# A trunk layer on one core: unit phases from two small tables, and the embedding, the first weight loads and a branch's number arranged anew around the routing

## The chip, the cores and the metric

The kernel runs on one core of one Trainium2 chip. The metric is the device time of one execution in microseconds (us). The profile is of one execution, and its times count from the start of that execution's span.

## The reference

One post-norm decoder layer for 512 tokens of 2048 features, in float32:

```python
z = x @ w_in + b_in                      # 2048 -> 1024 (u) + 1024 (v) + 1024 (g)
y_ssm = s5_group(u, lam, dt, b, c, d_skip, w_glu, b_glu)   # 64 groups, 64 complex states each
y_conv = conformer_conv_group(v, g, w_dw, ...)             # 31 taps per channel, LN, silu
y = concat([y_ssm, y_conv]) @ w_o + b_o
h = layer_norm(ALPHA * x + y, ln1_g, ln1_b)
m = hierarchical_moe(h, w_rg, w_re, w_gate, w_up, w_down)  # 32 experts, 2 per token
h = layer_norm(ALPHA * h + m, ln2_g, ln2_b)
e = (p @ w_p) * sigmoid(h @ w_pg + b_pg)                   # p: 512 x 256
x = layer_norm(ALPHA * h + e, ln3_g, ln3_b)
```

The state-space part is the recurrence s(t) = lam_bar * s(t-1) + B u(t) with complex lam_bar for each state, and y = Re(C s) + d_skip * u. The kernel works on it in blocks of 8 tokens: within a block it multiplies with tables of powers of lam_bar, and across the 64 blocks it scans the magnitudes alone, after the block states have been turned by unit phases exp(-i n theta), and turns them back behind the scan. `cc` and `ss` are the cosines and sines of these phases for block numbers n = 0..63.

## The kernel before, in words

The program is written in the order of its stages, and a planner reorders the instructions of each engine: it puts them on the engines by their waits and by costs that it assumes, so what stands next to what is its doing. Tiles come from pools; a new tile waits until the last reader of the buffer it takes is done.

Stages, in the profile's time:

- 0 to about 402: `x @ w_in` in 24 column tiles. Every float32 product is made of three matmuls of split operands (high x high, low x high, high x low; L100 to L102), for which ScalarE casts the high part (L79) and VectorE or GpSimd subtracts for the low part (L80). Eight SSM tiles of 128 channels, with their state-space work, alternate with tiles of the convolution, whose 31 taps run on VectorE (L234, L236). GpSimd makes the SSM tile's tables (`ssm_tables`, L439 to L454, with a scratch tile `big` of 128x1024). VectorE makes the phases: `phases(ft)` (L401 to L419) runs once for two SSM tiles and doubles six times, from 1 block number to 64; each doubling is six products or sums of 128x(8m) elements, m = 1, 2, 4 up to 32. For each tile ScalarE copies the half it needs into `pc` and `pz` (L496, L498), and VectorE multiplies with them around the scan (L525 to L534).
- 402 to 470: `w_glu`. The SSM outputs and the conv outputs went to DRAM (`z_dram`, `c_dram`) and are read back as `zraw` and `hcv`, on SP's queue.
- 470 to 677: `w_o`, LN1, and the logits of the router for the four token tiles (`logits`, L848 and L852). `tt` holds the four token tiles of h, which are also stored to `h_dram`.
- 677 to 733: `embedding()` computes p @ w_p for all tokens (L835), copies it on ScalarE (L836) and stores it to `p_dram` for the last stage (L838). It needs nothing from the layer, so it stands beside the last logits. Then the routing, in small VectorE instructions and matmuls (L950 to L1027): `cmax`, the number of rows that an expert has beyond the usual, goes into `tab`; slots and weights of the rows come from one-hot sums (L190, L196, L203).
- 726 to 1272: the experts, in 13 groups. A group gathers its rows of h from DRAM (GpSimd, L1059), transposes them (L1073), multiplies by gate and up weights (L1093), forms the activation, multiplies by the down weights (L1113) and scatters the result (L1063). The weights of an expert are 6 blocks of 1 MB (4 `w_gu`, 2 `w_dn`), 192 in all, loaded on SP's queue into a ring of 17 buffers (L1055), of which the last two are the `raw` buffers of the stages before. Group 0 has two fixed experts, 12 blocks; which experts the others have is read from `ids` into SP's registers (L1127). Behind group 0 stands a branch on `most` (the value of `cmax`, L1159), for the rows that don't fit; it isn't taken here.
- 1272 to the end: LN2, the gate product `h @ w_pg`, times `p_dram`, LN3.

Each DMA that SP or ScalarE issues takes the next of eight completion counters (lanes) in program order, and waits until the last transfer on that lane has landed. At a branch, SP waits for all eight.

Of the kernel before, what the change touches and what calls it, by code (L numbers as in the profile page):

```python
# [17 lines left out]
P = 128  # L18
# [36 lines left out]
def build(tc, I, out, dbg=None, stages=9):  # L55
# [188 lines left out]
    def bank(name, bufs=1):  # L244
        if name in bturn:

            n = bturn[name]
            bturn[name] += 1
            name, bufs = (("zp", 4) if n % 5 < 4 else ("xp", 1)) if name == "ops" else (("wps", "cps")[n % 2], 1)
        return psA.tile([P, 512], FT, name=name, tag=name, bufs=bufs)  # L250

    if True:
        with ExitStack() as s2:
# [136 lines left out]

            Cb = tpool.tile([P, 8, 4, 6], FT, name="Cb")
            Sb = tpool.tile([P, 8, 4, 6], FT, name="Sb")
            for dst, srct in ((Cb, cs), (Sb, sn)):
# [4 lines left out]

            def phases(ft):

                cc = tpool.tile([P, 8, NN], FT, name="cc")  # L401
                ss = tpool.tile([P, 8, NN], FT, name="ss")
                tm = vpool.tile([P, 8, NN // 2], FT, name="tm", tag="xr", bufs=1)
                G.memset(cc[:, :, 0:1], 1.0)
                G.memset(ss[:, :, 0:1], 0.0)
                bases = [t[:, ft:ft + 2].rearrange("p t g j -> p (t g) j") for t in (Cb, Sb)]
                for j in range(6):
                    m = 1 << j
                    cb_, sb_ = (b[:, :, j:j + 1].broadcast_to([P, 8, m]) for b in bases)
                    t_ = tm[:, :, 0:m]  # L410
                    c0, c1, s0, s1_ = cc[:, :, 0:m], cc[:, :, m:2 * m], ss[:, :, 0:m], ss[:, :, m:2 * m]
                    V.tensor_tensor(c1, c0, cb_, op=OP.mult)
                    V.tensor_tensor(t_, s0, sb_, op=OP.mult)
                    V.tensor_tensor(c1, c1, t_, op=OP.subtract)
                    V.tensor_tensor(s1_, s0, cb_, op=OP.mult)
                    V.tensor_tensor(t_, c0, sb_, op=OP.mult)
                    V.tensor_tensor(s1_, s1_, t_, op=OP.add)
                return cc, ss

            cs_pair = []  # L420
            setup.close()
# [3 lines left out]
            def ssm_tables(ft):  # L425
# [208 lines left out]
    if True:  # L634
# [146 lines left out]
        with ExitStack() as s3:  # L781
# [40 lines left out]

            def embedding():

                pT = wB.tile([P, 2, S], FT, name="pT", tag="whi", bufs=4)
                nc.sync.dma_start(pT, I["pT"])
                for q in range(2):
                    wp = raw_load(I["w_p"][q]).rearrange("p (k n) -> p k n", k=2)
                    for c in range(2):
                        for m in range(NT):  # L830
                            if m % 2 == 0:
                                pe_ = wB.tile([P, 2, 512], FT, name="pe", tag=("whi", "wlo")[m // 2], bufs=4)
                            ps = bank("ops")
                            for k in range(2):
                                T.matmul(ps, pT[:, k, m * P:(m + 1) * P], wp[:, k, c * 512:(c + 1) * 512], start=k == 0, stop=k == 1)  # L835
                            A.copy(pe_[:, m % 2], ps)  # L836
                            if m % 2:
                                A.dma_start(p_dram[m - 1:m + 1, 2 * q + c].rearrange("m p d -> p m d"), pe_)  # L838

# [37 lines left out]
            for c in range(4):  # L877
# [19 lines left out]
                else:  # L897
                    hls = [next(w_o) for q in range(2)]
                    for m in range(NT):
# [3 lines left out]
                        last = finish(m)  # L903
            embedding()

# [131 lines left out]
    if True:  # L1037
# [98 lines left out]

        early = [loads(0, q) for q in range(6)]
        for m in range(NT):
            A.mul(tt[m], tt[m], ALPHA)
# [3 lines left out]
        for i, (width, members) in enumerate(GROUPS):  # L1143
# [4 lines left out]
            for q in range(4):  # L1148
                up(gu, st, loads(i, q) if i else early[q], q)
            at = act(gu, wt0[:, i:i + 1])  # L1150
            if i + 1 < NGR and i:
                columns()
            for q in range(2):
                down(at, st, loads(i, 4 + q) if i else early[4 + q], q, sl0[:, NGR + i:NGR + i + 1])
# [282 lines left out]
```

## Time and profile before

| | us |
|---|---|
| median of 3 runs (range) | 1529.64 (1523.28 to 1530.3) |
| the profiled execution | 1528.31 |
| its span | 1526.6 |
| TensorE busy | 1260.8 |
| VectorE busy | 825.5 |
| ScalarE busy | 371.6 |
| GpSimd busy | 332.8 |
| DMA, mean over the span | 229 GB/s |

The busy time of an engine is a sum over stages in which different things set the end: the table says which engine has most to do, and not which one is waited for. For that the rows further down are taken by stretch of time, and the waits of an engine name what ended each of them. The engines are PE (TensorE), DVE (VectorE), ACT (ScalarE), POOL (GpSimd) and SP, which only issues transfers here; PEclk is the granted TensorE clock as a share of 2.4 GHz.

### The profile page before, as it was taken

What the parts mean: (1) busy time and instruction counts of PE and PEld (TensorE: products, weight loads), DVE (VectorE), ACT (ScalarE), POOL (GpSimd) and SP (SyncE); (2) the same over time, 40 slices, a digit from 0 to 9 for tenths busy, and PEclk for the clock granted to TensorE, in tenths of its full rate; (3) what the DMA queues carried; (4) which work ended last, traced back from release to release, by engine and by line L of the source; (5) the groups of instructions that cost most, each with busy time, mean ns of one, the idle gap of its engine ahead of it and who ended that gap; (6) DMA issues with size and microseconds to landing.
All of it is one profiled execution on the core that took longest, in us unless ns stands there. A gap on an engine that the chain in (4) does not pass through costs nothing. (4 is left out here: it accounts for less than half of the span.)

```text
span 1526.6 us, 16736 instructions
## 1 busy us (share of the span) xinstructions
PE 1260.8 (83%) x6206; PEld 806.8 (53%) x6207; DVE 825.5 (54%) x1369; ACT 371.6 (24%) x558; POOL 332.8 (22%) x273
## 2 busy tenths in 40 slices
PE   6988989899489999997639898977776766489996
PEld 4766768777368788874313332312211211378884
DVE  7999999969998934375101111100000005976567
ACT  4332634454243613122000111100000003023210
POOL 0444435373283520000001111100000003710000
PEclk9989889999799999998669999998889887689998
DMA  6333434433723235123899999999999996326312
GB/s 227 109 99 116 132 112 136 123 113 110 273 102 123 77 114 200 58 81 151 344 407 387 420 412 420 421 417 417 416 410 410 420 398 245 117 109 228 120 60 117
DMA packets 97497, 349.21 MB, mean 229 GB/s; under 512 B 29688, under 2 KB 43256, under 8 KB 61824
## 3 DMA queue, kind: packets, MB, share of 16 engines
q1 hardware_dynamic: 50880, 303.08, 51.2%
q10 hardware_dynamic: 40912, 28.20, 6.3%
q0 software_dynamic: 5616, 16.79, 2.8%
q8 instruction: 51, 0.84, 0.2%
q14 instruction: 38, 0.31, 0.1%
HBM read 323.17 MB, written 35.34 MB: 235 GB/s over the span
## 5 line engine op out<-in xcount | busy, mean ns | idle before, releaser
L1093 PE MATMUL gu<-ring,xt 128*32 128x512 f32 (+2 forms) x1144 | 234.8, 676 | 54.3 <-DMA ring<-w_gu 54.2
L236 DVE SCALAR_TENSOR_TENSOR cps<-hc,wdw,cps 128x512 f32<-128x512 f32 x232 | 174.0, 750 | 3.2
L100 PE MATMUL zp<-xh,whi 128*128 128x512 f32 x384 | 157.7, 412 | 10.7 <-ACT whi L79 10.1
L79 ACT CAST whi<-raw 128x1024 fp32r<-128x1024 f32 x116 | 119.4, 1046 | 177.6 <-PE zp L102 60.0
L1093 PEld LDWEIGHTS gu<-ring,xt 128*32 128x32 f32 (+2 forms) x1144 | 58.8, 128 | 194.7 <-issue 102.9
L102 PE MATMUL zp<-xh,wlo 128*128 128x512 f32 x384 | 156.0, 406 | 3.1 <-DVE wlo L80 3.1
L101 PE MATMUL zp<-xl,whi 128*128 128x512 f32 x384 | 156.5, 408 | 1.6 <-DVE xl L80 1.6
L80 DVE TENSOR_TENSOR wlo<-raw,whi 128x1024 fp32r<-128x1024 f32 x90 | 119.3, 1336 | 59.8 <-ACT whi L79 58.8
L1099 DVE TENSOR_TENSOR act<-act,gu 128x256 f32<-128x256 f32 x13 | 5.5, 422 | 259.1 <-ACT act L1098 259.1
L1113 PE MATMUL dps<-ring,at 128*32 128x512 f32 (+2 forms) x568 | 116.7, 625 | 10.7 <-ACT at L1104 5.5
L1063 POOL DMA_INDIRECT y_dram<-ob,sl x26 | 25.6, 986 | 364.7 <-ACT ob L1115 355.5
L100 PE MATMUL fps<-whi,h2h 128*128 128x512 f32 x224 | 89.6, 401 | 1.0 <-ACT h2h L79 1.0
L102 PE MATMUL fps<-whi,h2l 128*128 128x512 f32 x224 | 89.7, 401 | 0.0
L100 PEld LDWEIGHTS zp<-xh,whi 128*128 128x128 f32 x384 | 75.2, 196 | 26.2 <-ACT whi L79 9.8
L101 PE MATMUL fps<-wlo,h2h 128*128 128x512 f32 x224 | 88.9, 398 | 0.0
L1078 DVE COPY xt<-xtp 128x512 f32<-128x512 f32 x26 | 18.0, 692 | 128.5 <-PE xtp L1073 128.5
L102 PEld LDWEIGHTS zp<-xh,wlo 128*128 128x128 f32 x384 | 75.2, 196 | 20.9 <-DVE wlo L80 4.3
L80 POOL TENSOR_TENSOR wlo<-raw,whi 128x1024 fp32r<-128x1024 f32 x26 | 68.0, 2621 | 81.1 <-ACT whi L79 72.6
L101 PEld LDWEIGHTS zp<-xl,whi 128*128 128x128 f32 x384 | 75.3, 196 | 17.4 <-DVE xl L80 2.0
L1115 DVE COPY ob<-dps 128x512 f32<-128x512 f32 x26 | 18.0, 692 | 103.5 <-PE dps L1113 103.5
L1113 PEld LDWEIGHTS dps<-ring,at 128*32 128x32 f32 (+2 forms) x568 | 31.5, 122 | 79.6 <-issue 57.7
L1073 PE MATMUL xtp<-ident,gx 128*128 128x128 f32 x208 | 35.9, 298 | 39.1 <-DMA gx<-h_dram,sl 29.7
(434 smaller groups left out, 2287.1 us busy)
## 6 DMA issues: line engine op xcount, KB each, us to landing
ring<-w_gu SPq DMA_DIRECT2D x114, 1024.0 KB, 20.9
ring<-w_dn SPq DMA_DIRECT2D x56, 1024.0 KB, 20.6
raw<-w_in SPq DMA_DIRECT2D x24, 1024.0 KB, 5.5
raw<-w_o SPq DMA_DIRECT2D x16, 1024.0 KB, 4.8
raw<-w_gu SPq DMA_DIRECT2D x14, 1024.0 KB, 19.0
raw<-w_pg SPq DMA_DIRECT2D x14, 1024.0 KB, 5.8
raw<-w_dn SPq DMA_DIRECT2D x8, 1024.0 KB, 23.9
raw<-y_dram SPq DMA_DIRECT2D x12, 512.0 KB, 6.8
```

Source lines behind the costliest of these rows:

```text
L79: A.copy(hi, src)
L80: eng.tensor_tensor(lo, src, hi.bitcast(FT), op=OP.subtract)
L100: T.matmul(ps, lh, rh, start=start, stop=False)
L101: T.matmul(ps, lh, rl, start=False, stop=False)
L102: T.matmul(ps, ll, rh, start=False, stop=stop)
L236: V.scalar_tensor_tensor(ps if k < 30 else acc, hc[:, k:k + S], wdw[:, ct, k:k + 1], ps, op0=OP.mult, op1=OP.add)
L1063: G.indirect_dma_start(out=y_dram[q], out_offset=bass.IndirectOffsetOnAxis(ap=isc, axis=0), in_=ob[:, q * 1024:(q + 1) * 1024], in_offset= ...
L1073: T.transpose(ps[:, kk * P:(kk + 1) * P], gx[:, k * P:(k + 1) * P], ident)
L1078: V.tensor_copy(o, ps)
L1093: T.matmul(gu[cols], xt[:, k, cols], raws[j][:, kk * 512:(kk + 1) * 512], start=k == 0, stop=k == KD - 1)
L1113: T.matmul(outs[c][cols], at[:, k, cols], raws[j][:, o:o + 512], start=k == 0, stop=k == 1)
L1115: (A.copy if c else V.tensor_copy)(ob[:, q * 1024 + c * 512:q * 1024 + (c + 1) * 512], outs[c])
```

## The change

There are two halves.

The phases. `phases()` is gone. Ahead of the tiles VectorE makes two small tables for all 64 groups at once, `tc_` and `ts_` of [128, 2, 32, 8]: cosine and sine of n theta for n = 0..7, and of 8n theta for n = 0..7, by three doublings of six instructions. Each SSM tile then forms its `cc` and `ss` as products of the two tables, in six instructions of 128x256 on GpSimd (`E` is GpSimd), with `big` as the scratch. `Cb` and `Sb`, their base phases, move to another pool, and the scratch of the phases no longer shares a buffer with `xr`.

The routing's surroundings. `embedding` is made per token tile: a ScalarE copy of its part of p with an added zero z that is computed from a routing value, so that it can't start before this value: tile 0 behind the last logits, tile 1 behind `cmax`, tile 2 behind the weights `wt0`, and tile 3 behind group 0 of the experts (`pm3`). The branch's number is copied by VectorE into the first column of `xt` behind group 0, and read from there. Five blocks of group 1 are loaded ahead of the branch (`ahead1`): three into ring buffers, and two into the `raw` buffers, which hold `w_p` until tile 3's embedding is done and join the ring only then.

```diff
-            def phases(ft):
...
-                    V.tensor_tensor(c1, c0, cb_, op=OP.mult)
...
+            tc_, ts_ = (tpool.tile([P, 2, 32, 8], FT, name=n) for n in ("tc_", "ts_"))
...
+            for j in range(3):
...
+                V.tensor_tensor(c1, c0, cb_, op=OP.mult)
+                V.tensor_tensor(t_, s0, sb_, op=OP.mult)
+                V.tensor_tensor(c1, c1, t_, op=OP.subtract)
+                V.tensor_tensor(s1_, s0, cb_, op=OP.mult)
+                V.tensor_tensor(t_, c0, sb_, op=OP.mult)
+                V.tensor_tensor(s1_, s1_, t_, op=OP.add)
...
-                if ft % 2 == 0:
-                    cs_pair[:] = phases(ft)
-                cc, ss = (t[:, 4 * (ft % 2):4 * (ft % 2) + 4] for t in cs_pair)
...
+                E.tensor_tensor(cv, ch, cl, op=OP.mult)
+                E.tensor_tensor(tm, sh_, sl, op=OP.mult)
+                E.tensor_tensor(cv, cv, tm, op=OP.subtract)
+                E.tensor_tensor(sv, sh_, cl, op=OP.mult)
+                E.tensor_tensor(tm, ch, sl, op=OP.mult)
+                E.tensor_tensor(sv, sv, tm, op=OP.add)
...
-            def embedding():
...
+            def embedding(m, x):
+
+                z = op_.tile([P, 1], FT, name="pz0", bufs=1)
+                V.tensor_scalar(z, x, 0.0, 0.0, op0=OP.is_equal, op1=OP.mult)
+                pm = wB.tile([P, 2, P], FT, name="pm", tag="whi", bufs=4)
+                A.activation(pm, pT[:, :, m * P:(m + 1) * P], AF.Identity, bias=z)
...
-            embedding()
...
+            embedding(0, lg[:, NT - 1, 0:1])
...
+            embedding(1, cmax)
+            embedding(2, wt0[:, 0:1])
...
-        ring = [big(f"ring{n}") for n in range(2, NRING)] + [rpool.tile([P, D], FT, name="raw", tag="raw", bufs=2) for _ in range(2)]
+        ring = [big(f"ring{n}") for n in range(2, NRING)]
...
+            ahead1 = [loads(1, q) for q in range(3)]
+
+            for q in range(2):
+                pe_ = ep.tile([P, 2, 512], FT, name="pe")
...
+            ring.extend(rpool.tile([P, D], FT, name="raw", tag="raw", bufs=2) for _ in range(2))
+            ahead1 += [loads(1, q) for q in range(3, 5)]
...
-            most = nc.values_load(tab[0:1, 2 * NP:], min_val=0, max_val=S)
+            mo = xt[:, 0, 0:1].bitcast(I32)
+            V.tensor_copy(mo, tab[:, 2 * NP:])
+            most = nc.values_load(mo[0:1], min_val=0, max_val=S)
```

Where the instructions stand, at three places. The first is GpSimd's queue, from the end of one SSM tile's tables to the start of the next. Before:

```order
L454 TENSOR_TENSOR t_510<-t_510,big 128x1024
L404 MEMSET cc 128x8
L569 MEMSET hc 128x30
L439 TENSOR_TENSOR bw<-ba,qr 128x8x16
L442 TENSOR_TENSOR bw<-bb,qr 128x8x16
L441 TENSOR_TENSOR bw<-bw,sm 128x8x16
L405 MEMSET ss 128x8
L443 TENSOR_TENSOR sm<-ba,qi 128x128
L452 TENSOR_TENSOR wt<-Lr,bw 128x1024
L444 TENSOR_TENSOR bw<-bw,sm 128x8x16
```

And now (lines of the changed kernel; L448 to L450 are the products of the tables, L491 to L496 the phases):

```order
L450 TENSOR_TENSOR t_533<-t_533,big 128x1024
L492 TENSOR_TENSOR big<-ts__308 128x256
L493 TENSOR_TENSOR cc<-cc,big 128x256
L495 TENSOR_TENSOR big<-tc__307,ts__308 128x256
L496 TENSOR_TENSOR ss<-ss,big 128x256
L491 TENSOR_TENSOR cc<-tc__307 128x256
L494 TENSOR_TENSOR ss<-ts__308,tc__307 128x256
L573 MEMSET hc 128x30
L435 TENSOR_TENSOR bw<-ba,qr 128x8x16
L438 TENSOR_TENSOR bw<-bb,qr 128x8x16
```

The four remaining phase instructions of a tile stand behind its last table product, the first two of the next tile ahead of that tile's tables.

The second place is SP's queue at the end of the SSM tiles. `z_dram_85` is the last SSM tile's output, `c_dram_92` a conv tile's. Before:

```order
L650 DMA tt_3430<-x_tok 128x2048
L650 DMA tt_3431<-x_tok 128x2048
L650 DMA tt_3432<-x_tok 128x2048
L650 DMA tt_3433<-x_tok 128x2048
L75 DMA raw<-w_glu 128x2048
L561 DMA z_dram_85<-gl 128x512
L238 DMA c_dram_92<-acc 128x512
L608 DMA zraw<-z_dram_78 128x512
L608 DMA zraw<-z_dram_79 128x512
```

And now:

```order
L565 DMA z_dram_85<-gl 128x512
L612 DMA zraw<-z_dram_78 128x512
L612 DMA zraw<-z_dram_79 128x512
L612 DMA zraw<-z_dram_80 128x512
L612 DMA zraw<-z_dram_81 128x512
L612 DMA zraw<-z_dram_82 128x512
L612 DMA zraw<-z_dram_83 128x512
L612 DMA zraw<-z_dram_84 128x512
L612 DMA zraw<-z_dram_85 128x512
L615 DMA hcv<-c_dram_86 128x512
```

The conv store that stood between the last z store and the loads of z has moved behind them.

The third is TensorE's queue from the last logits to the first gather's transposes (L852 and L855 are the logits' matmuls, L835 and L839 the embedding, L950 and L958 the first routing matmul, L1073 and L1083 the transposes). Before:

```order
L835 MATMUL zp<-raw,pT 128x512 x4
L848 MATMUL wps<-ident,tt_3433 128x128 x4
L835 MATMUL zp<-raw,pT 128x512 x4
L835 MATMUL xp<-raw,pT 128x512
L852 MATMUL yp<-wr,scr 128x36 x4
L835 MATMUL xp<-raw,pT 128x512
L835 MATMUL zp<-raw,pT 128x512 x8
L852 MATMUL yp<-wr,scr 128x36 x4
L835 MATMUL xp<-raw,pT 128x512 x2
L835 MATMUL zp<-raw,pT 128x512 x6
L852 MATMUL yp<-wr,scr 128x36 x4
L950 MATMUL xp<-ones,scr 32x1 x4
```

And now, from the last matmuls ahead of `cmax`:

```order
L978 MATMUL zp<-scr,ones 128x32
L979 MATMUL xp<-ones,scr 32x1
L1028 MATMUL zp<-scr,ones 128x104
L839 MATMUL zp<-raw,pm 128x512 x6
L839 MATMUL xp<-raw,pm 128x512 x2
L196 MATMUL cps<-rsc_5391 128x26 x8
L203 MATMUL wps<-rsc_5391 128x13 x8
L839 MATMUL zp<-raw,pm 128x512 x8
L1083 MATMUL xtp<-ident,gx 128x128 x8
```

The embedding, which was mixed with the logits, now stands in pieces between the routing's matmuls: tile 0 ahead of the first (not shown), tile 1 ahead of the one-hot sums, tile 2 ahead of the transposes. On SP's queue the read of `tab` (L1159) that stood ahead of the 12 loads of group 0 is gone; the read of `xt` (L1186) stands behind them, behind three loads of group 1 and the reads of `ids`.

## Rows read from the trace of the kernel before

**Rows 1.** busy us by stretch: PE, PEld, DVE, ACT, POOL; PEclk, DMA, GB/s

```profile
100.00:200.00 100.00, 85.60 (x487) 68.92 (x486) 98.19 (x139) 43.54 (x67) 53.92 (x48) 0.90 0.43 126
200.00:300.00 100.00, 86.40 (x477) 71.75 (x475) 98.95 (x133) 45.48 (x71) 42.94 (x37) 0.94 0.42 123
300.00:400.00 100.00, 91.60 (x507) 75.88 (x506) 83.70 (x111) 45.69 (x71) 50.55 (x27) 0.94 0.42 126
```

**Rows 2.** busy us by stretch, columns as in the first group

```profile
720.00:740.00 20.00, 7.73 (x35) 7.40 (x34) 8.68 (x31) 0.00 (x0) 1.26 (x1) 0.50 0.63 250
762.70:1272.00 509.30, 389.44 (x2054) 119.00 (x2054) 45.63 (x75) 38.50 (x75) 37.07 (x37) 0.91 0.99 407
```

**Rows 3.** VectorE groups of `phases()`: count | busy us, mean ns | idle

```profile
L414 DVE TENSOR_TENSOR cc<-cc,tm 128x8 f32<-128x8 f32 (+5 forms) x24 | 17.4, 723 | 0.0
L413 DVE TENSOR_TENSOR tm<-ss,Sb 128x8 f32<-128x8 f32 (+5 forms) x24 | 16.3, 677 | 0.1
L416 DVE TENSOR_TENSOR tm<-cc,Sb 128x8 f32<-128x8 f32 (+5 forms) x24 | 14.7, 613 | 0.2
L412 DVE TENSOR_TENSOR cc<-cc,Cb 128x8 f32<-128x8 f32 (+5 forms) x24 | 11.0, 460 | 0.0
L417 DVE TENSOR_TENSOR ss<-ss,tm 128x8 f32<-128x8 f32 (+5 forms) x24 | 10.1, 419 | 0.0
L415 DVE TENSOR_TENSOR ss<-ss,Cb 128x8 f32<-128x8 f32 (+5 forms) x24 | 7.8, 323 | 0.0
```

**Rows 4.** timeline, VectorE, then GpSimd: start us, duration us, instruction

```profile
48.27 0.41 DVE L383 TENSOR_TENSOR Lr<-Lr 128x256 f32<-128x256 f32 x1
58.16 1.42 DVE L414 TENSOR_TENSOR cc<-cc,tm 128x8 f32<-128x8 f32 x1
...
57.51 2.04 POOL L452 TENSOR_TENSOR t<-Lr,ca 128x1024 f32<-128x1024 f32 x1
```

**Rows 5.** GpSimd groups by form: count | busy us, mean ns | idle

```profile
L670 POOL TENSOR_TENSOR near<-near,hcv 128x512 f32<-128x512 f32 x4 | 5.8, 1458 | 0.3
L441 POOL TENSOR_TENSOR bw<-bw,sm 128x128 f32<-128x128 f32 x8 | 4.5, 567 | 0.0
```

**Rows 6.** TensorE wait (total, times, longest); SP timeline; z store to landing

```profile
PE zp L100 <- ACT zh L79: 21.6, 1, 21.6
...
404.24 0.33 SPq L561 DMA_DIRECT2D z_dram<-gl  x1
414.40 0.33 SPq L238 DMA_DIRECT2D c_dram<-acc  x1
414.77 3.94 SPq L608 DMA_DIRECT2D zraw<-z_dram  x8
...
z_dram<-gl SPq DMA_DIRECT2D x8, 256.0 KB, 4.9
```

**Rows 7.** VectorE's wait for the logits; TensorE's timeline behind w_o

```profile
DVE la L856 <- PE yp L852: 13.7, 3, 7.3
...
693.24 7.03 PE L835 MATMUL zp<-raw,pT 128*128 128x512 f32 x16
...
715.18 0.56 PE L950 MATMUL xp<-ones,scr 128*32 128x1 f32 x8 [6.34 <-DVE scr L139]
```

**Rows 8.** SP: wait for the branch's number, timeline of loads, reads of `ids`

```profile
SPq L1159 <- DVE scr L989: 78.7, 1, 78.7
...
726.62 4.00 SPq L1055 DMA_DIRECT2D ring<-w_gu  x8
...
762.73 1.53 SPq L1055 DMA_DIRECT2D ring<-w_gu  x3
...
L1127 SPq TENSOR_LOAD <-ids x30: 261/266/284, 740.9 to 757.7; - x30
```

**Rows 9.** TensorE's timeline: down product of group 0

```profile
764.98 8.78 PE L1113 MATMUL dps<-ring,at 128*64 128x512 f32 x32 [0.46 <-ACT at L1104]
```

**Rows 10.** VectorE's timeline at the first use of the phases

```profile
102.00 0.69 DVE L525 TENSOR_TENSOR xr<-xp,pc 128x512 f32<-128x512 f32 x1 [0.34 <-ACT xs L523]
```

More of the change, by code (lines that the diff above doesn't have):

```diff
@@ L389, in build @@
             V.tensor_scalar(Li, Li, sig, None, op0=OP.mult)
-            Cb = tpool.tile([P, 8, 4, 6], FT, name="Cb")
-            Sb = tpool.tile([P, 8, 4, 6], FT, name="Sb")
+            Cb = spool.tile([P, 8, 4, 6], FT, name="Cb")
+            Sb = spool.tile([P, 8, 4, 6], FT, name="Sb")
             for dst, srct in ((Cb, cs), (Sb, sn)):
@@ L397, in build @@
                                   srct[ph, 1:7].rearrange("p j (t u g) -> p j t u g", t=8, u=2)[:, :, :, hf])
-            def phases(ft):
[L401 to L411, printed above, removed]
-                    V.tensor_tensor(c1, c0, cb_, op=OP.mult)
[L413 to L420, printed above, removed]
+            tc_, ts_ = (tpool.tile([P, 2, 32, 8], FT, name=n) for n in ("tc_", "ts_"))
+            V.memset(tc_[:, :, :, 0:1], 1.0)
+            V.memset(ts_[:, :, :, 0:1], 0.0)
+            tm_ = spool.tile([P, 2, 32, 4], FT, name="tm_")
+            bases = [t.rearrange("p t g (a j) -> p a (t g) j", a=2) for t in (Cb, Sb)]
+            for j in range(3):
+                m = 1 << j
+                cb_, sb_ = (b[:, :, :, j:j + 1].broadcast_to([P, 2, 32, m]) for b in bases)
+                t_ = tm_[:, :, :, 0:m]
+                c0, c1, s0, s1_ = (t[:, :, :, a:a + m] for t in (tc_, ts_) for a in (0, m))
+                V.tensor_tensor(c1, c0, cb_, op=OP.mult)
[4 more added lines that the diff above has]
+                V.tensor_tensor(s1_, s1_, t_, op=OP.add)
             setup.close()
@@ L821, in build @@
             V.tensor_reduce(kbc, kd_, axis=AX.X, op=OP.add)
-            def embedding():
-                pT = wB.tile([P, 2, S], FT, name="pT", tag="whi", bufs=4)
-                nc.sync.dma_start(pT, I["pT"])
+            def embedding(m, x):
[3 more added lines that the diff above has]
+                A.activation(pm, pT[:, :, m * P:(m + 1) * P], AF.Identity, bias=z)
                 for q in range(2):
-                    wp = raw_load(I["w_p"][q]).rearrange("p (k n) -> p k n", k=2)
+                    pe_ = wB.tile([P, 2, 512], FT, name="pe", tag="wlo", bufs=4)
                     for c in range(2):
[L830 to L838, printed above, removed]
+                        ps = bank("ops")
+                        for k in range(2):
+                            T.matmul(ps, pm[:, k], wps[q][:, k, c * 512:(c + 1) * 512], start=k == 0, stop=k == 1)
+                        A.copy(pe_[:, c], ps)
+                    A.dma_start(p_dram[m, 2 * q:2 * q + 2].rearrange("c p d -> p c d"), pe_)
             def logits(m, c):
@@ L903, in build @@
                         last = finish(m)
-            embedding()
+            pT = wB.tile([P, 2, S], FT, name="pT", tag="whi", bufs=4)
+            nc.sync.dma_start(pT, I["pT"])
+            wps = []
+            for q in range(2):
+                wps.append(raw_load(I["w_p"][q]).rearrange("p (k n) -> p k n", k=2))
+            embedding(0, lg[:, NT - 1, 0:1])
             rp = Carve(scr)
@@ L1137, in build @@
         early = [loads(0, q) for q in range(6)]
+        pm3 = ep.tile([P, 2, P], FT, name="pm3")
+        nc.sync.dma_start(pm3, I["pT"][:, :, (NT - 1) * P:])
         for m in range(NT):
@@ L1148, in build @@
             for q in range(4):
-                up(gu, st, loads(i, q) if i else early[q], q)
+                up(gu, st, early[q] if i == 0 else ahead1[q] if i == 1 else loads(i, q), q)
             at = act(gu, wt0[:, i:i + 1])
@@ L1153, in build @@
             for q in range(2):
-                down(at, st, loads(i, 4 + q) if i else early[4 + q], q, sl0[:, NGR + i:NGR + i + 1])
+                down(at, st, early[4 + q] if i == 0 else ahead1[4] if (i, q) == (1, 0) else loads(i, 4 + q), q, sl0[:, NGR + i:NGR + i + 1])
             if i:
                 continue
-            most = nc.values_load(tab[0:1, 2 * NP:], min_val=0, max_val=S)
+            ahead1 = [loads(1, q) for q in range(3)]
+            for q in range(2):
+                pe_ = ep.tile([P, 2, 512], FT, name="pe")
+                for c in range(2):
+                    ps = bank("dps", 4)
+                    for k in range(2):
+                        T.matmul(ps, pm3[:, k], wps[q][:, k, c * 512:(c + 1) * 512], start=k == 0, stop=k == 1)
+                    (A.copy if c else V.tensor_copy)(pe_[:, c], ps)
+                A.dma_start(p_dram[NT - 1, 2 * q:2 * q + 2].rearrange("c p d -> p c d"), pe_)
+            ring.extend(rpool.tile([P, D], FT, name="raw", tag="raw", bufs=2) for _ in range(2))
[3 more added lines that the diff above has]
+            most = nc.values_load(mo[0:1], min_val=0, max_val=S)
             with tc.If(most > 0):
```

5 lines of the change are left out of this document (added).

## The prediction, made before the changed kernel was run

> **What bounds the kernel now.** I read the busy times by stretch first, since a share over the whole span mixes stages with different limits. Between 100 and 300 us VectorE is busy 98.2 and 99.0 us of each 100, TensorE 85.6 and 86.4 at a granted clock of 0.90 and 0.94; between 300 and 400 it is 83.7 against 91.6 [rows 1]. So up to about 300 us VectorE sets the pace and TensorE waits in pieces; near 400 us they are close. In the expert stage the DMA share is 0.99 over 509.3 us at 407 GB/s [rows 2]: of the 192 weight blocks (32 experts, 6 each) 180 are loaded there, and what counts is when the stream can start and how much is left. The change touches both stages, and nothing between 417 and 677 or behind 1272 us but for shifting it.
>
> **Phases: what VectorE loses.** The six lines of `phases()` cost 17.4, 16.3, 14.7, 11.0, 10.1 and 7.8 us, each 24 instructions: 77.3 us [rows 3]. They are dear for their size: a 128x8 subtraction takes 1.42 us at 58.16, while a GpSimd multiplication of 2.04 us runs from 57.51 [rows 4]; it ends with the GpSimd instruction, not after its own work. A free 128x256 product takes 0.41 us [rows 4].
>
> What is added on VectorE is 18 instructions of 64 to 256 elements for the two small tables. At 0.41 or less each that is at most 7.4 us; sizes below 256 are cheaper, and I take 6 us. If each met a GpSimd instruction as the one at 58.16 did, it would be 18 x 1.42 = 26 us.
>
> On GpSimd six instructions of 128x256 per tile are added, 48 in all, and 8 small memsets go. The size isn't in the trace; between 0.57 us for 128x128 and 1.46 us for 128x512 [rows 5] I take 0.8, near the geometric middle: 38 us, with ends of 27 and 70. They lie beside other work, as GpSimd is busy 54, 43 and 51 us of each 100 [rows 1]. But they hold VectorE up in the way just read. Each of the 48 can at worst cost VectorE its length (38 us), at best nothing; half an instruction's length in about half of the cases is 48 x 0.4 x 0.5 = 10 us, which I take. VectorE's relief is 77.3 - 6 - 10 = 61 us, with ends of 77.3 - 26 - 38 = 13 and 77.3 - 6 = 71.
>
> That row and a rule agree on the mechanism and differ on its extent. The Trainium skill, "SBUF — State Buffer", section "Who interferes with whom", says that a VectorE instruction with two SBUF inputs and a GpSimd instruction that reads SBUF shut each other out for a whole instruction; its "GPSIMD Engine Reference", section "Engine selection", would keep elementwise work on VectorE. By the rule at its fullest the relief would be 77.3 - 6 - 38 = 33 us; that is the third rival below.
>
> **Phases: what reaches the end.** TensorE can't return more than it loses: 14.4 + 13.6 + 8.4 = 36.4 us idle between 100 and 400 us, and at a clock of 0.90, 0.94 and 0.94 at most 10 + 6 + 6 = 22 us of slow running [rows 1], of which some is counted in the idle time already (the clock stands low in a stall too); I take 14. Of these 50 us I give half to the change, 25: VectorE keeps the conv taps and the splits, and the waits on round trips through DRAM remain. The ends are 8 and 50.
>
> **The same half moves a store.** TensorE waits 21.6 us for the first `zh` cast behind the last SSM tile [rows 6]. The last z store is issued at 404.24, but on SP the next instruction is a store of the convolution, which has to wait for VectorE's taps until 414.40, and only behind it come the eight loads of z at 414.77 [rows 6]. In the new order the eight loads stand right behind the z store, and the conv store later. The store still has to land, 4.9 us in the median [rows 6], against the 10.2 us of being held: 5 us come back, between 0 (the loads queue behind a 1 MB weight block) and 10. First half in all: -30 us.
>
> **Embedding, taken out of the logits' way.** Now the 64 rows of p@w_p share TensorE with the last logits; VectorE waits 13.7 us for `yp` there [rows 7], and the routing's first matmul runs at 715.18 [rows 7]. Without it the last logits come up to 13.7 us earlier. But `embedding(0)` then stands in front of that first matmul in TensorE's queue: 16 rows, 7.03 us at the full clock [rows 7], with ScalarE's gated copy ahead of it. It runs from about 697.5 to 708, so the routing gains 715.2 - 708 = 7 us (between 4 and 11). `embedding(1)`, gated by `cmax`, stands in front of the one-hot sums (L196): another 7 us at full and up to 14 at half speed, in a stretch in which the clock is granted at 0.50, that is 1.2 GHz [rows 2]. That eats the gain: the gather of group 0 goes out between 2 us earlier and 2 us later than before. `embedding(2)` hides behind the gather's flight and leaves TensorE warm for group 0, worth some 2 us. Group 0's last matmuls end at 764.98 + 8.78 = 773.8 before [rows 9]; I put them at 770 (767 to 773).
>
> **Loads, read late in name only.** SP's wait of 78.7 us on the branch's number [rows 8] disappears, and nothing of the number holds the 12 loads of group 0 any more, which began at 726.62 [rows 8]. Yet each load takes the next of eight completion lanes in turn, shared with ScalarE's stores, and waits until the lane's last transfer landed. The fourth waits for the store of `sv`, which follows `cmax`; the fifth and sixth for stores of `embedding(1)`, the seventh and eighth for those of `embedding(2)`, about 741 us; the w_dn blocks need buffers that `embedding(2)` reads. So most of the 12 go out no earlier than before, some 10 us later.
>
> Then SP reads its ids (30 of them from 740.9 to 757.7 before [rows 8]), and has 5 blocks of group 1 ahead of the branch. The last two of them overwrite w_p and so wait for the last token tile's embedding, which stands behind group 0 on TensorE: 770 + 7 = 777 us. At the branch SP waits for every lane. Two blocks of 1.05 MB at 407 GB/s take 2.6 us each [rows 2], and 2 us for the start and the end of a transfer (a quarter of a block takes 4.9 us in all [rows 6]): SP goes on at about 784, between 776 and 792. Before it went on at 762.73 [rows 8], with 5 blocks fewer loaded. The end of the stream, which has no other slack, moves by 784 - 762.7 - 5 x 2.6 = +8 us, between 0 and +16. The 7 us on TensorE behind group 0 cost nothing themselves, as it waits for group 1's gather there.
>
> **The sum** against the profiled execution's 1528.31 us (1.3 below the median): 1528.3 - 25 - 5 + 8 = 1506 us.
>
> **Rivals.**
> 1. VectorE's relief returns all of TensorE's loss: -50 - 8 + 8, 1478 us. For it speaks a VectorE that is never idle from 100 to 300 us; against it that several of TensorE's stalls end with a DMA or ScalarE's casts. 0.13.
> 2. The second half gains too: the whole 13.7 us stay because both embeddings find TensorE idle anyway, group 0 ends at 760 and SP goes on at 774, which is -2. Then -30 - 2, 1496 us. Against it: `embedding(0)` and `embedding(1)` stand in front of the routing's matmuls in TensorE's queue. 0.10.
> 3. The lockout at its fullest: relief 33 us, of which the added GpSimd time keeps TensorE from the tables it waits for, so that the first half brings some 10 us in all and the second takes 8: 1526 us, no change. 0.15.
> 4. Slower: the phases come too late. Before, they were made for two tiles at once and well ahead. Now four of a tile's six instructions stand behind its tables in GpSimd's queue, and four ScalarE copies behind those, about 4 x 0.8 + 4 x 0.8 = 6.4 us per tile; if VectorE reaches L525 sooner than that, it stops, with the splits for TensorE queued behind it. Eight tiles at 6.4 us are 51 us: -30 + 51 + 8, 1557 us. It decides from 22 / 8 = 2.8 us per tile. Against it: at 102.00 L525 waits 0.34 us, for ScalarE's `xs` and not for the phases [rows 10], and GpSimd is idle half of the time. 0.10.
>
> **How the numbers follow.** The forecast has 0.52, with its own range of 1490 to 1521. A measurement of this kernel tells about 0.5% (7.6 us) from no change. Faster by more: 0.52 + 0.13 + 0.10, less a little for the forecast's upper edge: 0.74. Within: the third rival and that edge, 0.15. Slower: 0.11. Eight times in ten the time lies between 1478 (the first rival) and 1528 (the third, with the late end of the stream); the fourth is left out.
>
> **What the new profile should show.** VectorE some 55 to 65 us less busy before 400 us, GpSimd some 30 to 45 us more; TensorE less idle between 100 and 400 us, with the last `zh` wait below 17 us. The first routing matmul some 7 us nearer to the last w_o matmul; L196 behind embedding rows at a low clock; SP's restart behind the branch some 20 us later than before, measured from the last w_o matmul. I am wrong on the first half if VectorE's busy time falls and TensorE's idle time doesn't; on the second if SP goes on within 13 us of where it did, so that the stream ends no later.

## The result, and the profile of the changed kernel

The changed kernel takes 1479.72 us (median of 4 runs, 1478.26 to 1482.75), a ratio of 0.9694 to the kernel before (0.9672 to 0.9715): 47 us faster by the ratio, twice the 22 that were forecast. The profiled execution took 1482.75 us, 45.6 less than that of before.

A table of landmarks tells which stage gave what. They are start times of TensorE instructions in the profiled executions:

| | before | changed | moved by | forecast |
|---|---|---|---|---|
| last `w_in` matmul (L100) | 395.8 | 373.1 | -22.7 | -25 |
| first matmul on z behind it | 418.2 | 373.8 | -21.7 more | -5 |
| last `w_o` matmul | 676.6 | 631.1 | -1.1 more | 0 |
| last down product of the experts | 1272.13 | 1227.93 | +1.3 | +8 |
| end of the span | 1526.6 | 1480.9 | -1.5 more | 0 |

The stretches that answer to [rows 1], changed kernel: busy us of PE, PEld, DVE, ACT, POOL, then PEclk, DMA share, GB/s.

```profile
100.00:200.00 100.00, 96.37 (x556) 79.87 (x555) 90.18 (x99) 51.57 (x84) 72.82 (x65) 0.95 0.42 124
200.00:300.00 100.00, 95.41 (x561) 79.38 (x561) 89.37 (x102) 53.32 (x86) 74.95 (x64) 0.95 0.48 141
300.00:400.00 100.00, 94.89 (x464) 78.56 (x464) 90.74 (x103) 45.28 (x68) 62.08 (x36) 0.93 0.56 193
```

TensorE is at 95 to 96 us of each 100 where it was at 86 to 92, VectorE is no longer full, and GpSimd has 12 to 32 us more. The two kinds of new instructions, one row of each kind (the page's groups by form: count | busy us, mean ns):

```profile
L410 DVE TENSOR_TENSOR tc__307<-tc__307,Cb 128x256 f32<-128x256 f32 x1 | 0.5, 475 | 0.0
...
L496 POOL TENSOR_TENSOR ss<-ss,big 128x256 f32<-128x256 f32 x8 | 9.3, 1159 | 0.6
```

The 18 small-table instructions take 6.5 us together. The six groups of products on GpSimd take 48.4 us, 1.01 us each.

SP's queue around the last z store, which answers to [rows 6]:

```profile
357.40 0.33 SPq L238 DMA_DIRECT2D c_dram<-acc  x1
361.45 0.33 SPq L565 DMA_DIRECT2D z_dram<-gl  x1
361.87 4.30 SPq L612 DMA_DIRECT2D zraw<-z_dram  x8
```

The last z is stored at 361.45, 12 us before the last `w_in` matmul begins; before, it was stored at 404.24, 8 us behind it. The wait of 21.6 us for the first cast of z is gone from TensorE's list altogether.

SP's and TensorE's timelines around the routing, which answer to [rows 7 to 9]:

```profile
651.12 44.24 SPq L1065 DMA_DIRECT2D ring<-w_gu  x8
695.46 2.30 SPq L1065 DMA_DIRECT2D ring<-w_dn  x4
...
722.25 0.35 SPq L1065 DMA_DIRECT2D raw<-w_gu  x1
725.68 0.33 SPq L1065 DMA_DIRECT2D raw<-w_dn  x1
734.25 0.35 SPq L1065 DMA_DIRECT2D ring<-w_dn  x1
...
659.60 0.41 PE L958 MATMUL zp<-ones,scr 128*32 128x1 f32 x8
...
668.72 7.14 PE L839 MATMUL zp<-raw,pm 128*128 128x512 f32 x12 [4.50 <-ACT pm L833]
...
711.50 7.09 PE L1123 MATMUL dps<-ring,at 128*64 128x512 f32 x32 [0.46 <-ACT at L1114]
718.52 7.13 PE L1177 MATMUL dps<-raw,pm 128*128 128x512 f32 x16
```

Eight loads of group 0 are spread over 44 us, since each waits for a lane (SP waited 49.0 us for a store of `h_dram` ahead of the first, and among the eight 34.9 us for six stores of `p_dram` and 6.4 us for the store of `sv_dram`); the two raw loads stand behind the last embedding matmuls, and the first load behind the branch goes out at 734.25.

### The profile page after: what moved, and what is told of

Same layout as the page of the kernel before. It is cut to its first block, busy times and chain, and to the rows that moved or that the text cites. A ratio compares the mean times of both kernels' runs of the same rounds, so it can differ in the third digit from the quotient of the medians.

```text
span 1480.9 us, 16676 instructions
## 1 busy us (share of the span) xinstructions
PE 1262.3 (85%) x6206; PEld 805.9 (54%) x6207; DVE 778.5 (53%) x1251; ACT 372.5 (25%) x559; POOL 382.7 (26%) x313
## 5 line engine op out<-in xcount | busy, mean ns | idle before, releaser
L1103 PE MATMUL gu<-ring,xt 128*32 128x512 f32 (+2 forms) x1144 | 237.9, 671 | 58.7 <-DMA ring<-w_gu 58.7
L100 PE MATMUL zp<-xh,whi 128*128 128x512 f32 x384 | 157.5, 411 | 11.3 <-ACT whi L79 10.2
L80 DVE TENSOR_TENSOR wlo<-raw,whi 128x1024 fp32r<-128x1024 f32 x90 | 123.8, 1386 | 55.3 <-ACT whi L79 54.4
L1123 PE MATMUL dps<-ring,at 128*32 128x512 f32 (+2 forms) x568 | 113.6, 612 | 12.1 <-DMA ring<-w_dn 7.0
L1073 POOL DMA_INDIRECT y_dram<-ob,sl x26 | 25.6, 985 | 367.6 <-ACT ob L1125 358.0
L80 POOL TENSOR_TENSOR wlo<-raw,whi 128x1024 fp32r<-128x1024 f32 x26 | 72.4, 2787 | 85.8 <-ACT whi L79 73.3
L100 PE MATMUL fps<-whi,h2h 128*128 128x512 f32 x224 | 89.2, 399 | 0.7 <-ACT h2h L79 0.7
L100 PEld LDWEIGHTS zp<-xh,whi 128*128 128x128 f32 x384 | 74.6, 194 | 26.0 <-ACT whi L79 10.3
L101 PEld LDWEIGHTS zp<-xl,whi 128*128 128x128 f32 x384 | 74.6, 194 | 16.8 <-DVE xl L80 2.0
L1069 POOL DMA_INDIRECT gx<-h_dram,sl x13 | 13.7, 1052 | 195.9 <-PE xtp L1083 133.2
```

The costliest lines, as they stand in the source:

```text
L80: eng.tensor_tensor(lo, src, hi.bitcast(FT), op=OP.subtract)
L100: T.matmul(ps, lh, rh, start=start, stop=False)
L101: T.matmul(ps, lh, rl, start=False, stop=False)
L1073: G.indirect_dma_start(out=y_dram[q], out_offset=bass.IndirectOffsetOnAxis(ap=isc, axis=0), in_=ob[:, q * 1024:(q + 1) * 1024], in_offset= ...
L1103: T.matmul(gu[cols], xt[:, k, cols], raws[j][:, kk * 512:(kk + 1) * 512], start=k == 0, stop=k == KD - 1)
L1123: T.matmul(outs[c][cols], at[:, k, cols], raws[j][:, o:o + 512], start=k == 0, stop=k == 1)
```

## The experiments

Two questions were open: which half gave the surplus, and why the wait for z went. A third came up on the way: why the end of the expert stage moved so little in either direction.

**The halves apart.** One kernel has the first half of the diff alone, the other the second half alone:

```diff
-                if ft % 2 == 0:
-                    cs_pair[:] = phases(ft)
+                E.tensor_tensor(cv, ch, cl, op=OP.mult)
...
```

```diff
-            embedding()
+            embedding(0, lg[:, NT - 1, 0:1])
...
```

> The first half alone (small tables and products on GpSimd); embedding, loads and branch as before. Theory: the whole gain comes from this half. The trace of the changed kernel puts the last w_o matmul 45.5 us earlier and the last expert matmul 44.2 us earlier, so this kernel should take about 1528.3 - 45.5 = 1483 us (1479 to 1487), 0.970 of before, and its expert stage should be that of before. Rival: the halves are about what was forecast (-30 and a loss of 8) and something of the second half helps the first stages, through the order; then 1498 us.

> The second half alone (embedding per token tile, early loads, late read of the number, five blocks ahead of the branch); phases as before. Theory: it takes the stream's end by 1 to 2 us later and the last stage 1 us shorter, so 1528 us, within 3 us of before. Rival, the prediction's term: 8 us slower, 1536 us. The wait for the first cast of z should be 21 to 22 us, as before, since nothing of the first stages is changed.

Measured: the first half alone 1482.68 us, 0.971 of before (0.9682 to 0.9737); the second alone 1525.01 us, 0.9995 (0.9985 to 1.0004). The whole gain is the first half's, within what the two intervals tell, and the second is worth nothing, neither the forecast loss of 8 us nor a gain. The first half alone has the new order of the z loads and no wait for z (last `w_in` matmul at 373.2, first on z at 373.9); the second alone keeps that wait, with 20.9 us, and its last down product comes 596.6 us behind the last `w_o` matmul, against 595.5 before.

**The wait for z, from the side of SP's order.** The kernel before, with the conv stores on another queue:

```diff
-            nc.sync.dma_start(c_dram[ct], acc)
+            G.dma_start(c_dram[ct], acc)
```

> The kernel before with one edit: the stores of the convolution's tiles are issued by GpSimd and not by SP, so that the loads of z stand right behind the last z store on SP's queue and no store that waits for VectorE's taps stands between. Tells apart what the order on SP was worth and what VectorE's queue was worth in the stall of 21.6 us. Theory A (order on SP, 10.2 us held, less the store's landing): the stall falls to 14 to 17 us and the time by 5 to 8 us, to about 1522. Theory B (the stall is SP's doing altogether): it falls below 8 us, the time by 14 us or more. Theory C (it is all VectorE's queue): no change. In the changed kernel the last z store is issued 12 us before the last w_in matmul, in the kernel before 8 us after it; by that 20 us of the stall belong to the engine that makes z, and I hold A.

TensorE's wait and SP's timeline in that kernel:

```profile
PE zp L100 <- ACT zh L79: 6.7, 1, 6.7
...
400.66 0.33 SPq L561 DMA_DIRECT2D z_dram<-gl  x1
401.19 3.96 SPq L608 DMA_DIRECT2D zraw<-z_dram  x8
```

The loads go out 0.5 us behind the z store, and the wait falls by 15 us to 6.7: 10 of them are the hold (from the last z store to the first matmul on z it is 4.1 us, 400.66 to 404.8, and was 14.0), and the other 5 aren't the order's: the last z was stored 3.6 us earlier, and the last `w_in` matmul ran 1.5 us later (397.3). 1520.16 us is measured (0.9969, 0.9955 to 0.9983): 5 us faster. By the wait it is nearer to the theory that SP's order makes it all (below 8 us) than to the one I held; by the time it is the one I held, because the next stage gives half of it back: from the first matmul on z to the last `w_o` matmul it takes 265.2 us and not 258.4. Of these 6.8 us, 2.6 are a longer wait (6.6 us, 4.0 before) for the normalised conv output (`hcv`), which needs the taps that VectorE hasn't done; in the others TensorE is busy, part of the time at a lower granted clock (0.94 from 454.5 to 564.6 us, where it was 1.00 from 473.3 to 571.2). Moving the loads alone hands much of the stall on.

**The wait for z, from the side of VectorE's load.** The changed kernel, with 15 idle reductions per SSM tile on VectorE:

```diff
+                idle = tpool.tile([P, 1], FT, name="idle")
+                for _ in range(15):
+                    V.tensor_reduce(idle, tc_.rearrange("p a g b -> p (a g b)"), axis=AX.X, op=OP.add)
```

> The changed kernel with the load given back to VectorE: 15 reductions of 128x512 per SSM tile, of some 0.65 us each, whose result nobody reads (8 x 15 x 0.65 = 78 us, what the old phases took). Tells apart whether the wait for the first cast of z went because VectorE's queue is shorter or because of where the instructions stand. Theory (VectorE's load): nearly all of the first half's gain goes, 1518 to 1530 us, and the wait for the first cast of z is back with 10 to 22 us. Rival (the new order does it): the time rises by no more than what VectorE holds up in front of the last w_in matmul, 20 to 25 us, to 1500 to 1506 us, and the wait for z stays under 3 us.

```profile
PE zp L100 <- ACT zh L79: 17.8, 1, 17.8
...
386.41 0.33 SPq L568 DMA_DIRECT2D z_dram<-gl  x1
386.79 7.65 SPq L615 DMA_DIRECT2D zraw<-z_dram  x6
401.32 0.32 SPq L238 DMA_DIRECT2D c_dram<-acc  x1
401.68 0.92 SPq L615 DMA_DIRECT2D zraw<-z_dram  x2
```

1506.25 us (0.985, 0.9807 to 0.9893; the profiled execution is one of the longer ones, 1511.02). The reductions took 80.8 us, and VectorE was busier over the span than before the change (836.2 against 825.5 us). Neither theory came out whole. The wait for z is back with 17.8 us, a conv store stands in front of two of the z loads again, and the `hcv` wait is back with 5.5 (none in the changed kernel): these follow VectorE's load. But the last `w_in` matmul starts at 376.3, only 3 us later than without the load. So the 22.7 us by which the `w_in` stage became shorter don't come from VectorE's total.

**The products on the other engine, twice, and not at all.** The first exchanges the engine, the second repeats the six instructions, the third leaves them out:

```diff
-                E.tensor_tensor(cv, ch, cl, op=OP.mult)
+                V.tensor_tensor(cv, ch, cl, op=OP.mult)
...
```

> The changed kernel with the 48 products of the two tables on VectorE in place of GpSimd. They take 0.42 us each there where no GpSimd instruction is in the way, so VectorE gets 20 us (up to 35 with waits for GpSimd's lock) and GpSimd loses 48 us. Theory (VectorE's load decides): the time goes up by about a third of that, 7 to 12 us, to 1487 to 1492 us. Rival (the lock decides: GpSimd's 48 us cost VectorE as much as doing it itself): no change, within 3 us of 1480, or faster.

> The changed kernel with each of the 48 products on GpSimd made twice (48 us more GpSimd work, same values). It prices GpSimd's time in VectorE's: the prediction put 10 us of VectorE time on 38 us of GpSimd time, the measured busy times put some 24 us on 48. Theory (lock): VectorE's busy time up to 400 us rises by 10 to 24 us, the time by 5 to 12 us, to 1485 to 1492 us. Rival (GpSimd is idle enough and VectorE has idle time now): no change, within 2 us of 1480. Second rival (phases too late, each tile held 8 us): 1530 us and more.

> The changed kernel with the 48 products left out: cosine and sine are set to 1 and 0 by two GpSimd memsets per tile, so the phases are missing from the result. It is the floor of the first half. Theory (what is left in front of the last w_in matmul is TensorE's own work): little is left to gain, 2 to 8 us, 1472 to 1478 us. Rival (VectorE still sets the pace and GpSimd's products cost it 24 us): 12 us or more, 1468 us or less.

| | last `w_in` matmul | last `w_o` matmul | time, us | ratio (95%) |
|---|---|---|---|---|
| changed | 373.1 | 631.1 | 1479.72 | 0.9694 (0.9672 to 0.9715) |
| products on VectorE | 376.4 | 636.2 | 1488.91 | 0.9769 (0.9746 to 0.9793) |
| products twice on GpSimd | 390.0 | 649.5 | 1501.0 | 0.9837 (0.9814 to 0.986) |
| no products | 358.2 | 624.2 | 1478.99 | 0.9698 (0.9678 to 0.9718) |

With the products on VectorE the time is 9 us above the changed kernel's, as the theory had it. So by the ratios the small tables are worth 35 of the 47 us (2.3 of 3.1%) with no help from GpSimd, and the engine the rest.

Products twice cost 21 us for some 46 us more on GpSimd, and 1501 us meets none of the three expectations. Two things grew. VectorE's busy time over the span rose by 16.8 us (795.3 against 778.5), and without the products it fell by 15.5 (763.0): GpSimd's products cost VectorE a third of their own time. And ScalarE waited for the copies of the phases:

```profile
ACT pc L505 <- POOL cc L499: 20.9, 6, 5.3
```

In the changed kernel this wait is 4.2 us. This is the chain from GpSimd over ScalarE to VectorE's scan, the mechanism of the prediction's fourth rival. Both together are 21 / 8 = 2.6 us per tile; how much of it each has, no run separates. (Up to 400 us VectorE's busy time is no larger than in the changed kernel, 325.3 against 329.3 us from 40 us on, but the slower kernel has done less by then.)

Without products the last `w_in` matmul is another 15 us earlier, but only 7 of these reach the last `w_o` matmul (TensorE's waits between the two sum to 9.2 us there and to 4.2 in the changed kernel), and none the median, within what the medians tell (a few us). The theory nearly held by its time (1478.99 us, 1 us above its range) and not by its reason: TensorE isn't at its floor in the `w_in` stage, but what is gained there is given back behind it.

**The branch and the raw loads.** In the changed kernel SP goes on at 734.25, 23 us behind its last early load. Three kernels try to have it earlier: the two raw loads behind the branch; the last tile's embedding ahead of group 0; and the embedding in one piece as before, with the late read and the five early blocks kept.

```diff
-            ahead1 += [loads(1, q) for q in range(3, 5)]
```

```diff
             embedding(2, wt0[:, 0:1])
+            embedding(3, wt0[:, 0:1])
...
-                        T.matmul(ps, pm3[:, k], wps[q][:, k, c * 512:(c + 1) * 512], start=k == 0, stop=k == 1)
...
```

```diff
-            embedding(1, cmax)
-            embedding(2, wt0[:, 0:1])
...
+            embedding()
...
```

> The changed kernel with the two loads into the raw buffers issued behind the branch and not ahead of it: three blocks of group 1 stand ahead of it in place of five. In the changed kernel these two were issued at 722.25 and 725.68 us, behind the last token tile's embedding, and SP went on behind the branch only at 734.25, when they had landed. Theory (the stream's end follows SP's start): the two are issued at about the same time, nothing is waited for, the next load goes out at about 726 in place of 734, and the time falls by 8 us to about 1472 us. Rival (the stream is held by group 1's gather and by buffers, not by SP's start): no change, within 2 us of 1480.

> The changed kernel with the last token tile's embedding made with the third's, behind the routing's weights, and not behind group 0: the two raw buffers are free some 20 us sooner, and group 0 starts some 7 us later, since 16 more embedding rows stand in front of its transposes. Theory (SP's start counts): SP goes on at about 720 in place of 734, and the time falls by 8 to 14 us, to 1466 to 1472 us. Rival (group 0's own end counts, through the scatter, the branch and group 1's gather): 5 to 7 us slower, 1485 to 1487 us.

> The changed kernel with the embedding as before (in one piece beside the last logits) and everything else as changed: the number is read late, five blocks of group 1 are loaded ahead of the branch, and no part of the embedding stands behind the routing or group 0. Theory, fitted on five kernels so far: the last expert matmul ends at SP's first load behind the branch plus 2.82 us for each block still to load. SP can go on when it has read the ids and the number, at about 89 us behind the last w_o matmul (before: 85; changed: 102), with 175 blocks left: 17 + 1 us less than in the changed kernel at best, and 14 less than with the first half alone: 1464 to 1470 us. Rival (the ring's buffers come free only with group 0 and group 1, so an earlier start finds nothing to fill): within 3 us of 1480.

They took 1484.02, 1485.41 and 1484.56 us (0.9726, 0.974, 0.9726; the intervals reach from 0.9705 to 0.9763). None is faster than the changed kernel. In the first and third neither the theory nor the rival came out; in the second the theory failed and the rival held (1485 to 1487). The first load behind the branch went out at 730.37, 735.76 and 712.68. In the first, SP stood at the branch from 721.3 to 730.1, where a store of the last embedding, issued at 724.45, had still to land, and won 5 us against the last `w_o` matmul for two blocks more to load; in the second it read its ids until 730.3 and stood at the branch until 735.5. So the rule "first load plus 2.82 us per block left" holds for both: 730.37 + 177 x 2.82 = 1229.5 (1228.96 in the trace) and 735.76 + 175 x 2.82 = 1229.3 (1228.31).

The third is the one that breaks it: 712.68 + 175 x 2.82 = 1206 against 1223.46. SP's waits and a stretch of that kernel:

```profile
SPq L1059 <- PE gu L1097: 51.1, 10, 27.7
...
740.00:760.00 20.00, 11.03 (x28) 5.75 (x29) 1.38 (x2) 0.58 (x1) 0.00 (x0) 0.63 0.51 207
...
737.84 1.03 POOL L1063 DMA_INDIRECT gx<-h_dram,sl  x1 [9.83 <-issue]
```

The ring is full: SP waits 51.1 us for buffers that TensorE has to free, the DMA share falls to 0.51, and TensorE waits 22.1 us for group 1's gather, which GpSimd issues behind the branch, where it stood until 736.5 (the last scatter of group 0 was issued at 727.03). So two things may share the bound here, and one alone gives nothing. The last two kernels issue group 1's gather ahead of the branch (and again at the end of the branch's body, which uses that buffer), on the third kernel and on the changed one:

```diff
+            gather(sl0[:, 1:2])
             mo = xt[:, 0, 0:1].bitcast(I32)
...
-            gather(sl0[:, 1:2])
+                gather(sl0[:, 1:2])
             columns()
```

> The kernel with the old embedding and the late number, and group 1's gather issued ahead of the branch (and once more at the end of the branch's body). There SP went on at 712.68 us but ran out of free buffers: the ring was full, the DMA share fell to 0.51 between 740 and 760 us, and TensorE waited for group 1's gather, which GpSimd issued at 737.84 behind the branch. Theory (two things share the bound: SP's start and the gather behind the branch): with both early the stream isn't starved, the last expert matmul comes at about 713 + 175 x 2.82 = 1207 us in place of 1223, and the time is 1465 to 1470 us. Rival (something else in groups 0 and 1 holds the ring): no change from that kernel, 1480 to 1485 us.

> The changed kernel with group 1's gather ahead of the branch alone. There SP goes on only at 734 us, so by the same rule (SP's first load plus 2.82 us per block left) the end of the stream should not move by more than 2 us: 1477 to 1482 us. Rival (the gather behind the branch is the bound by itself): 8 us or more faster, 1472 us.

On the third kernel it gives 1472.2 us, 0.9639 (0.9619 to 0.966): faster than both kernels of this case, 7.5 us less than the changed one. On the changed one it gives 1482.14, 0.972 (0.9703 to 0.9736): nothing, as expected. The gather in the faster kernel:

```profile
712.87 0.99 POOL L1063 DMA_INDIRECT gx<-h_dram,sl  x1 [21.42 <-PE xtp L1077]
```

Its last down product (1218.97) comes 585.7 us behind the last `w_o` matmul; in the eleven others and the two kernels of this case that distance lies between 593.0 and 598.3. The 1207 us that I expected were not reached. SP went on at 717.09, which gives 1210.6 by the rule, so 8 us are still held. The trace shows where: TensorE stands idle for 11.3 us between group 0's down product and group 1's transposes (730.8 to 742.05), no longer for the gather, which was issued 29 us earlier, but for a release that the profile doesn't name; GpSimd stands at the branch until 741.7. That the branch itself holds them is not tested.

## Why the prediction was wrong, point by point

**What bounds the kernel:** right for both stages, with one reservation. I read VectorE's 98 and 99 us as the bound up to 300 us and its busy time as the currency of the gain. The idle reductions and the products on VectorE show that its total can be given back (344 and 348 of the 360 us from 40 to 400, against 340.7 before) with the last `w_in` matmul 3 us later only. What had held TensorE was not that VectorE was full but what stood in it. TensorE's waits from 40 to 398 us sum to 34.4 us before and to 13.3 in the changed kernel (13.4 with the idle reductions, apart from the wait for z): 21 of the 22.7 us. The largest of those that went is the wait for `yb`, ScalarE's copy of an SSM tile's output:

```profile
PE yp L540 <- ACT yb L548: 12.4, 3, 7.4
...
120.83 0.39 PE L541 MATMUL yp<-sc,t 128*128 128x63 f32 x2
...
152.36 0.41 DVE L417 TENSOR_TENSOR ss<-ss,tm 128x256 f32<-128x256 f32 x1
...
154.49 0.59 ACT L548 COPY yb<-yp 128x512 f32<-128x512 f32 x1
```

The first tile's output was finished at 121 and copied 33 us later, behind the phases of the third and fourth tile. These were 36 instructions in six doublings, each on the one before. Their scratch `tm` lay in the one buffer that `yb` takes too (L417 is its last reader), and ScalarE's copies of the phases stood ahead of the copy to `yb`. In the changed kernel this copy comes 0.7 us behind the last matmul. So the old phases held TensorE by a chain and by a buffer, and the change takes away both, a thing that the prediction doesn't count. What each was worth, and whether they are all of the 22.7 us, is argued from the trace and not shown by a kernel of its own (the old phases with a scratch of their own would tell).

**VectorE's relief, 61 us:** the removed 77.3 and the added 6 were right (6.5). GpSimd's products were dearer, 1.01 us each and not 0.8. VectorE's busy time over the span fell by 825.5 - 778.5 = 47.0 us (46.6 with the first half alone), so other instructions on it grew by 77.3 - 6.5 - 47.0 = 24 us, where I had 10 for the lock, and 47 us are less than the 55 to 65 that I expected to see. Of the 24, 15.5 go with the products (the kernel without them); the other 8 are there without them too, and no run shows where they come from. By the rule of the Trainium skill ("SBUF — State Buffer", "Who interferes with whom") at its fullest, VectorE would have lost all of GpSimd's 48.4 us. The runs show a third of that: 15.5 us for the 48 products, and 16.8 for the second 48.

**What reaches the last `w_in` matmul, 25 us:** 22.7 measured. That the number held is luck as far as the reason goes: I halved TensorE's loss because VectorE keeps the taps and the splits, and the load isn't what counted.

**The z store, 5 us: this is the step that failed.** It gave 21.7, and is 16.7 of the some 23 us by which the trace gained more than the forecast (6.7 more are the end of the stream, below). I counted the 10.2 us in which SP was held, less a landing, and left the time at which the last z is ready where it stood, 8 us behind the last `w_in` matmul. The 22.4 us between that matmul and the first one on z were 8.4 to the last z store, 10.5 to the loads, and 3.4 to the matmul. To take off a landing was wrong by itself: with the conv store on another queue the hold gave back its 10 us in full. The rest, 12 us, is z itself. It is made on VectorE, by the same queue that I had just relieved; it came 20 us earlier against TensorE's matmuls, and then the whole wait was hidden beneath them. The two terms were not independent: the relief that shortens the stage also takes from what VectorE has left to do at its end, and TensorE waits for that. The reductions show the one half of it (load back, z 10 us behind the last `w_in` matmul again and 17.8 us of wait back) and the moved conv store the other (10 us of hold).

**Embedding and routing:** the first routing matmul gained 10 us against the last `w_o` matmul (28.5 us behind it, before 38.6), within the 4 to 11. `embedding(1)` ate less of it than I had: the gather went out 7 us earlier, outside of the 2 us that I gave it, since the rows ran for 9 us (668.7 to 677.6) and L196 behind them took 1.86 us at a granted clock of 1.00 (677.4 to 681.1), where it had taken 3.59 at 0.50 [rows 2]. I had expected it behind them at a low clock. Group 0's last matmuls ended at 718.6, 10 us nearer to the last `w_o` matmul, and not 4.

**The loads and SP's restart:** the mechanism was right (lanes, raw buffers, the last embedding, all lanes at the branch). SP went on 103 us behind the last `w_o` matmul, 17 later than before, where I had 21.

**The end of the stream, +8:** measured +1.3 in the trace and 0 in the time. Besides those 4 us the price of a block was too low: 2.6 us by bytes, but 509.4 / 180 = 2.83 before and 493.7 / 175 = 2.82 now, a price in which the gathers and scatters of the stretch are contained. 17 - 5 x 2.83 = 3; the other 2 us are the 175 blocks, each a little cheaper than before.

**The rivals:** the time fell to where the first rival had put it (1478), by another way: the `w_in` stage returned what the forecast gave, not all of TensorE's loss. The low end of the range was that rival, and the median lies inside it by 2 us; what was missed is the size of the forecast, 22 us against 47. The third (the lock at its fullest) and the fourth (phases too late) didn't happen, but the doubled products cost 2.6 us per tile, in part by the fourth's mechanism: the kernel stands near to it.

## What to carry to other kernels

Where an engine is relieved over a whole stage, ask what of its backlog another engine waits for at the stage's end, and count that wait as part of the same gain and not as a term of its own. When a bound stream is to start earlier, look for the second thing that frees its buffers: here neither SP's earlier start (with the old embedding) nor the earlier gather gave anything, and both together gave 7.5 us. Before an engine's busy time is taken as the currency of a gain, look in the other engine's waits for what stands in front of it, shared buffers too. And price a block of a shared stream by the stretch in which it ran, span by blocks, not by its bytes.

## What the runs showed of the hardware

A gather's flight depends on whether the weight stream is running. Group 1's gather was issued at 785.53 in the kernel before, 23 us behind SP's first load behind the branch, and at 732.95 in the changed one, 1.3 us ahead of it:

```profile
785.53 9.95 DMA gx<-h_dram,sl
...
732.95 6.09 DMA gx<-h_dram,sl
```

In five kernels with the gather 1.0 to 3.4 us ahead of that load (changed, products on VectorE, products twice, idle reductions, no products) it took 6.0 to 6.2 us, and 7.9 in the last of them; in five with it level or behind (before, first half alone, raw loads behind the branch, last tile early, old embedding) 9.7 to 12.0 us.

A product of 128x256 on GpSimd took 0.89 to 1.16 us in the mean of its line in the changed kernel, and 0.69 to 1.30 over all kernels that have these lines; the same six lines on VectorE take 0.41 to 0.71 us. With the idle reductions, which read one operand, on VectorE beside them, the six lines took 0.69 to 0.93 on GpSimd. So the same instruction's time there changes by what VectorE runs meanwhile.
